# Block sums of resident operands made beforehand, in pieces, and the last item's evacuations ahead of the rows behind it

## The chip, the cores and the metric

The kernel runs on one core of a Trainium2 chip. A core has five engines that work through their own lists of instructions in order: TensorE (PE, matrix products, with its weight loads listed as PEld), VectorE (DVE), ScalarE (ACT), GpSimd (POOL) and SyncE (SP), which issues most transfers. Waiting between engines goes by semaphores. Transfers (DMA) move data between device memory (DRAM tensors in the program) and the on-chip memory, and TensorE writes its results into banks of a separate accumulator memory (PSUM). The metric is device time in microseconds of one execution.

## The reference

One residual layer on a sequence of 2,048 positions with 1,024 channels: a mixer (eight heads of attention with forget gates beside a gated MLP on chunks of 128 positions), a dense SwiGLU network with 2,816 hidden channels, and a final norm.

```python
for l in range(DEPTH):                                    # DEPTH = 1
    xn = rms_norm(x, mix_norm_g[l])
    h = xn @ w_in[l]
    ...                                                   # attention and spatial gating
    x = x + merged @ w_out[l]
    xn = rms_norm(x, ffn_norm_g[l])
    gate, up = jnp.split(xn @ w_gate_up[l], 2, axis=-1)
    x = x + (jax.nn.silu(gate) * up) @ w_down[l]
return rms_norm(x, final_norm_g)
```

The change touches only the last four lines, the feed-forward part. Everything is float32; the kernel writes each float32 operand as a high half (a cast) and a low half (the rest), and makes a product of two such operands as three matmuls (high-high, high-low, low-high).

## The kernel before

The feed-forward part is the second half of the program, from about 1,098 us to the end. It works on *sets*: sets 1 and 2 are the gate-and-up products for the first and the second half of the positions (22 items each, one item per 128 hidden channels), sets 3, 4 and 5 the down product, cut into three blocks of hidden channels (8 items each, an item being two tiles of 128 positions). Two items at a time make a *group*; only the last two groups have one item each. Counted from 0, set 1 is groups 0 to 10, set 2 is 11 to 21, set 3 is 22 to 25, set 4 is 26 to 29 and set 5 is 30 to 34.

Within an item the product of two matrices is done by blocks, two by two, with seven block products in place of eight (Winograd's scheme). Each product n, from 0 to 6, takes one *moving-side* operand from the item's own stream (tiles `wh`, `wl`, made from the loaded tiles `raw`, `rawd`) and one *resident* operand that stays for the whole set (R0 to R6, each with a high and a low half; R0, R2, R5 and R6 live in the long tiles named `wh` and `wl` of 4,096 columns, R1, R3 and R4 in tiles of their own). Some of these operands are blocks of the matrices, others are sums of blocks. `stream` makes the sums and halves of an item. `refill` makes the resident ones of the next set while the last group of the current set runs: after product n of that group its resident operand is free, and the next set's operand n is written in its place (`keep_as`: a cast on ScalarE, line 128, and a low half on VectorE, line 131, both over 2,048 columns).

Before the change, the four blocks of the next set lie in four staging slots `sg0` to `sg3` of 1 MB each (loaded at lines 1327 and 1331), and the block sums are made there in place, on VectorE (line 1343, 128x2048; one of those for set 5 on GpSimd): one at product 4 of the group before the last, three in the last group, between the casts:

```python
yield keep(0, b11)
tt(te[1], b11, b11, b12, ALU.add)
yield keep(1, b11)
yield keep(2, b21)
tt(te[2], b21, b21, b11, ALU.subtract)
tt(te[3], b11, b22, b11, ALU.subtract)
yield keep(3, b11)
```

Order is set by the program's own loop over (group, product) slots and by a scheduler that places each engine's instructions; every engine then runs its list in order. Moving-side operands are made ahead of TensorE, up to six (item, product) pairs (`LW = 6`), in six buffers for each half. Results leave PSUM in `evac`: for sets 1 and 2 (class `Up`) into `u`, `c` and `hT`, stored to DRAM at line 1472 (`HD`), for sets 3 to 5 (class `Down` on `Rows`) into rows of x that are loaded at line 1404 and stored at 1510. In set 5 a finished row is squared (line 1506), its reciprocal root is taken (VectorE at line 177, GpSimd at 179), it is scaled (line 1531) and stored (line 1532). These steps (`done`) wait in a list `posts`, and the main loop takes one step per item and product. The last matmuls are those of group 34, and the rows of group 33 finish beside it.

Lines that the prediction names: 1654 is the matmul of all seven products, 1409 and 1411 the evacuation of products 0 and 1 of a row item, 1414, 1416, 1418, 1421 and 1424 that of products 2 to 6; 1439 and 1484 load an item's raw tiles, 1466 and 1470 are GpSimd's products of the gate.

## Time and profile before

| | us |
|---|---|
| three runs | 2388.26 to 2390.97, median 2390.56 |
| the profiled execution | 2384.64 |
| its span, first to last instruction | 2382.8 |
| TensorE busy | 2338.7 (98%) |
| VectorE busy | 1671.5 (70%) |
| ScalarE busy | 1055.9 (44%) |
| GpSimd busy | 627.4 (26%) |
| granted TensorE clock, mean | 0.995 of full |

The transfers move 380.6 MB at a mean of 160 GB/s. Shares are averages over stages that differ: what counts is the busy time of each engine group by group, and which wait ends last where TensorE stands idle. Matmul records overlap, since a matmul starts before the one ahead of it has ended; so a full TensorE is read from the distance of starts, or from the count of matmuls in a window.

### The profile page before, as it was taken

What the parts mean: (1) busy time and instruction counts of PE and PEld (TensorE: products, weight loads), DVE (VectorE), ACT (ScalarE), POOL (GpSimd) and SP (SyncE); (2) the same over time, 40 slices, a digit from 0 to 9 for tenths busy, and PEclk for the clock granted to TensorE, in tenths of its full rate; (3) what the DMA queues carried; (4) which work ended last, traced back from release to release, by engine and by line L of the source; (5) the groups of instructions that cost most, each with busy time, mean ns of one, the idle gap of its engine ahead of it and who ended that gap; (6) DMA issues with size and microseconds to landing.
All of it is one profiled execution on the core that took longest, in us unless ns stands there. A gap on an engine that the chain in (4) does not pass through costs nothing. (4 is left out here: it accounts for less than half of the span.)

```text
span 2382.8 us, 31420 instructions
## 1 busy us (share of the span) xinstructions
PE 2338.7 (98%) x10582; PEld 1893.8 (79%) x10582; DVE 1671.5 (70%) x2736; ACT 1055.9 (44%) x1770; POOL 627.4 (26%) x705
## 2 busy tenths in 40 slices
PE   9999999999999999999999999999999999999997
PEld 7777777777777767888888888788888878888886
DVE  6658658888888666567655656965555696696888
ACT  5322137777778766344323233432323242332433
POOL 1100002122111222221322323232322335364531
PEclk9999999999999999999999999999999999999999
DMA  7845567566587876666233232433232245455453
GB/s 256 286 154 202 196 210 196 165 164 178 154 222 234 225 224 172 211 223 201 71 89 89 80 95 75 153 85 89 72 89 81 81 140 187 167 185 202 152 188 148
DMA packets 358152, 380.60 MB, mean 160 GB/s; under 512 B 22292, under 2 KB 275924, under 8 KB 355432
## 3 DMA queue, kind: packets, MB, share of 16 engines
q1 hardware_dynamic: 342008, 335.36, 46.4%
q0 software_dynamic: 7616, 27.33, 3.3%
q10 hardware_dynamic: 8368, 15.91, 1.8%
q8 instruction: 85, 1.39, 0.2%
q14 instruction: 75, 0.61, 0.1%
HBM read 253.35 MB, written 125.18 MB: 159 GB/s over the span
## 5 line engine op out<-in xcount | busy, mean ns | idle before, releaser
L128 ACT CAST wh<-raw 128x512 fp32r<-128x512 f32 (+2 forms) x492 | 302.3, 621 | 752.7 <-PE pp L1654 607.9
L131 DVE TENSOR_TENSOR wl<-raw,wh 128x512 fp32r<-128x512 f32 (+2 forms) x496 | 374.9, 766 | 80.2 <-ACT wh L128 79.8
L1654 PE MATMUL pp<-wl,wh 128*128 128x512 f32 x1056 | 325.5, 389 | 1.4 <-ACT u L1409 1.2
L1654 PE MATMUL pp<-wh,wh 128*128 128x512 f32 x1056 | 325.3, 389 | 0.0
L1343 POOL TENSOR_TENSOR raw<-raw 128x512 f32<-128x512 f32 (+1 forms) x124 | 165.5, 1336 | 514.9 <-DMA raw<-in_w_gu_dram 334.9
L131 DVE TENSOR_TENSOR Pl<-Pt,Ph 128x512 fp32r<-128x512 f32 (+1 forms) x320 | 194.6, 613 | 79.1 <-ACT Ph L128 76.4
L1654 PEld LDWEIGHTS pp<-wl,wh 128*128 128x128 f32 x1056 | 198.0, 188 | 43.6 <-ACT u L1409 2.1
L1654 PEld LDWEIGHTS pp<-wh,wh 128*128 128x128 f32 x1056 | 198.2, 188 | 41.1
L732 ACT ACTIVATE Pt<-mx_ps 128x512 f32<-128x512 f32 (+1 forms) x320 | 169.3, 534 | 121.6 <-PE mx_ps L730 117.6
L1654 PE MATMUL pp<-wl,wl 128*128 128x512 f32 x528 | 205.7, 390 | 1.0 <-DVE wl L131 0.9
L1654 PE MATMUL pp<-wh,wl 128*128 128x512 f32 x528 | 205.4, 389 | 0.0
L921 PE MATMUL z<-wh,xz 128*128 128x512 f32 x496 | 188.9, 397 | 0.0
L1343 DVE TENSOR_TENSOR raw<-raw,raw 128x512 f32<-128x512 f32 (+1 forms) x112 | 133.8, 1197 | 77.4 <-POOL raw L1343 73.9
L128 ACT CAST Ph<-Pt 128x512 fp32r<-128x512 f32 (+1 forms) x320 | 175.8, 557 | 19.6 <-PE tp L764 3.8
L365 DVE TENSOR_REDUCE mx<-mx_ps 128x1 f32<-128x512 f32 x192 | 130.2, 682 | 23.9 <-PE mx_ps L363 20.4
L742 POOL TENSOR_SCALAR_AFFINE_SELECT Ph<-Ph 128x128 fp32r<-128x128 f32 x128 | 53.0, 414 | 323.0 <-DVE Pl L131 218.6
L363 PE MATMUL mx_ps<-D,A 66*128 66x512 f32 (+2 forms) x320 | 119.6, 376 | 5.7 <-DMA D<-KH 3.0
L762 PE MATMUL tp<-Ph,V 128*128 128x512 f32 (+1 forms) x320 | 118.6, 371 | 4.5 <-POOL Ph L742 3.6
L729 PE MATMUL mx_ps<-A,D 74*128 74x512 f32 (+1 forms) x320 | 118.9, 372 | 2.2 <-ACT Pt L732 2.2
L767 PE MATMUL tp<-Pl,V 128*128 128x512 f32 (+1 forms) x320 | 118.5, 370 | 1.2 <-POOL Pl L742 0.7
L1654 PEld LDWEIGHTS pp<-wl,wl 128*128 128x128 f32 x528 | 99.1, 188 | 22.6 <-DVE wl L131 2.1
L730 PE MATMUL mx_ps<-B,C 128*128 128x512 f32 (+1 forms) x320 | 116.9, 366 | 0.0
(340 smaller groups left out, 5300.9 us busy)
## 6 DMA issues: line engine op xcount, KB each, us to landing
raw<-in_w_gu_dram SPq DMA_DIRECT2D x88, 512.0 KB
xz<-XS SPq DMA_DIRECT2D x31, 1024.0 KB
HD<-hT SPq DMA_DIRECT2D x44, 512.0 KB
D<-KH SPq DMA_DIRECT2D x112, 128.0 KB
XA<-xa SPq DMA_DIRECT2D x27, 512.0 KB
raw<-HD SPq DMA_DIRECT2D x24, 512.0 KB
XA<-xb SPq DMA_DIRECT2D x21, 512.0 KB
xa<-XA SPq DMA_DIRECT2D x20, 512.0 KB
```

The costliest lines, as they stand in the source:

```text
L128: return nc.scalar.copy(o, i) if eng is nc.scalar else eng.tensor_copy(o, i)
L131: return eng.tensor_tensor(o, i, f(h), ALU.subtract)
L363: last_mx.append(nc.tensor.matmul(pm[:, 0:n], lhs, Dt[0 : lhs.shape[0], 0:n], start=True, stop=True))
L365: nc.vector.tensor_reduce(mx[:, a, s : s + 1], pm, AX.X, ALU.max)
L729: nc.tensor.matmul(st[:, off:], Dt[:, b * P : (b + 1) * P], A[:, off:], start=True, stop=False)
L730: nc.tensor.matmul(st[:, off:], C[:, b * P : (b + 1) * P], B[:, off:], start=False, stop=True)
L732: nc.scalar.activation(Pt[:, off:], st[:, off:], AF.Exp)
L762: nc.tensor.matmul(pv[:, off:], V[:, 0:P], Ph[:, off:], start=kb == 0, stop=False)
L767: nc.tensor.matmul(pv[:, off:], V[:, 0:P], Pl[:, off:], start=False, stop=kb == 4 * j + 3)
L921: nc.tensor.matmul(pz, xz[a][:, k, :], w[b][:, k, :], start=n == 0, stop=n == 3 * KT - 1)
L1343: (nc.vector if e == "v" else nc.gpsimd).tensor_tensor(o, a, b, op)
L1654: nc.tensor.matmul(pm, a[:, k, :], b[:, k, :], start=on is None and k == 0 and e == 0, stop=k == it.kh - 1 and e == 2, skip_group_check=n ...
```

## The change

The block sums of sets 2 to 5 are no longer made in the staging slots. A generator `block_sums` makes them beforehand, in 15 pieces (four for sets 2, 3 and 4, three for set 5), one in each of the groups 1 to 15: it loads a piece of 512 columns of each of the four blocks (256 KB each) into two tiles `xa`, makes four sums on VectorE (128x512), and stores the two tiles to new DRAM tensors `SM` (512 KB each), behind the group's two output stores. In the slot loop, the next set's slots are filled with operands 0 to 3, which are now either a block or a stored sum; in the last group, `refill` only casts and takes low halves, and after each of operands 0, 1 and 2 loads operand 4, 5 or 6 into the slot that has just been read.

For the last group alone, the steps of finished rows are taken in other numbers per product (two each for products 0 to 3, none for product 4, one for 5 and 6), they are placed behind the product's evacuation (`behind`), and in that group a row's reciprocal root and its scaling become two steps.

```diff
@@ -53,7 +53,6 @@
 NF_ = 6
 RL = 2
 SQ = 'p'
-TE = ['vvvv', 'vvpv', 'vvvv', 'vvvv', 'vvvv', 'vvpv']
 SE = 'pvpv'
 NY = 4
 NR = 5
@@ -1319,19 +1318,74 @@
     def stage():
         return [T(pers, [P, 4, CH], F32, f"sg{n}") for n in range(4)]
 
+    def block(s, i):
+
+        if s < 3:
+            return XT[s - 1][i]
+        kh, r0 = KB[s - 3] // 2, sum(KB[: s - 3])
+        r0 = (r0 + (i // 2) * kh) * P
+        return w_down[r0 : r0 + kh * P, (i % 2) * CH : (i % 2 + 1) * CH].rearrange("(k p) n -> p k n", p=P)
+
     def staged(s):
 
         sg = stage()
         for i, t in enumerate(sg):
-            if s < 3:
-                ld(t, XT[s - 1][i])
-                continue
-            kh, r0 = KB[s - 3] // 2, sum(KB[: s - 3])
-            r0 = (r0 + (i // 2) * kh) * P
-            ld(t[:, 0:kh, :],
-               w_down[r0 : r0 + kh * P, (i % 2) * CH : (i % 2 + 1) * CH].rearrange("(k p) n -> p k n", p=P))
+            ld(t, block(s, i))
         return sg
 
+    SM = {s: T(dram, [P, 4, 4, CH], F32, f"SM{s}") for s in (2, 3, 4, 5)}
+
+    def source(s, n):
+
+        if n in (0, 2, 6):
+            return block(s, {0: 0, 2: 2, 6: 3}[n])
+        return SM[s][:, {1: 0, 4: 1, 5: 2, 3: 3}[n], 0 : sets[s - 1][0].kh]
+
+    def fetch(s, n):
+
+        t = T(pers, [P, 4, CH], F32, f"sg{n % 4}")[:, 0 : sets[s - 1][0].kh]
+        ld(t, source(s, n))
+        return t
+
+    hd = []
+
+    def block_sums():
+
+        last = None
+        for s in (2, 3, 4, 5):
+            for k in range(sets[s - 1][0].kh):
+                n = yield
+                while n != 2:
+                    n = yield
+                if last:
+                    with behind(hd[-1]):
+                        put(*last)
+                while n != 3:
+                    n = yield
+                t = [T(xap, [P, D], F32, "xa") for _ in range(2)]
+                b = [t[i // 2][:, (i % 2) * CH : (i % 2 + 1) * CH] for i in range(4)]
+                with behind(*hd[-1:]):
+                    for i in range(4):
+                        ld(b[i], block(s, i)[:, k])
+                while n != 5:
+                    n = yield
+                tt("v", b[1], b[3], b[1], ALU.subtract)
+                tt("v", b[0], b[0], b[1], ALU.add)
+                n = yield
+                tt("v", b[2], b[2], b[0], ALU.subtract)
+                tt("v", b[3], b[3], b[0], ALU.subtract)
+                last = s, k, t
+        while n != 2:
+            n = yield
+        with behind(hd[-1]):
+            put(*last)
+        yield
+
+    def put(s, k, t):
+        for a in range(2):
+            ld(SM[s][:, 2 * a : 2 * a + 2, k], t[a].rearrange("p (c n) -> p c n", c=2))
@@ -1340,7 +1394,7 @@
     JOIN = {2: 0, 6: 3}
 
     def tt(e, o, a, b, op):
-        (nc.vector if e == "v" else nc.gpsimd).tensor_tensor(o, a, b, op)
+        return (nc.vector if e == "v" else nc.gpsimd).tensor_tensor(o, a, b, op)
 
     def keep_as(i, src, kh=4):
         rh, rl = resident(i)
@@ -1348,23 +1402,14 @@
         lo_of(nc.vector, rl[:, 0:kh, :], src, rh[:, 0:kh, :])
         return rh, rl
 
-    def refill(sg, kh, te):
-
-        b11, b12, b21, b22 = (t[:, 0:kh, :] for t in sg)
-
-        def keep(i, src):
-            return keep_as(i, src, kh)
-
-        yield keep(0, b11)
-        tt(te[1], b11, b11, b12, ALU.add)
-        yield keep(1, b11)
-        yield keep(2, b21)
-        tt(te[2], b21, b21, b11, ALU.subtract)
-        tt(te[3], b11, b22, b11, ALU.subtract)
-        yield keep(3, b11)
-        yield keep(4, b12)
-        yield keep(5, b21)
-        yield keep(6, b22)
+    def refill(s, sg):
+
+        kh = sets[s - 1][0].kh
+        for n in range(7):
+            r = keep_as(n, sg[n], kh)
+            if n < 3:
+                sg.append(fetch(s, n + 4))
+            yield r
 
     def stream(a11, a12, a21, a22):
 
@@ -1409,19 +1454,19 @@
                 copies.append(nc.scalar.copy(u, ps[0]))
             elif n == 1:
                 nc.vector.tensor_tensor(u, u, ps[1], ALU.add)
-                tt(self.adder, x[0][1], x[0][1], u, ALU.add)
+                self.last = tt(self.adder, x[0][1], x[0][1], u, ALU.add)
...
             for m in {5: (1,), 6: (0,)}.get(n, ()):
                 posts.append(self.done(2 * self.tp + m, self.x[m], now[0]))
 
@@ -1469,8 +1514,8 @@
                 nc.scalar.activation(h1, u, AF.Silu)
                 nc.gpsimd.tensor_tensor(h1, h1, c, ALU.mult)
                 kb, r = [(i, j) for i in range(3) for j in range(KB[i])][self.fi]
-                ld(HD[kb][self.half * 8 : (self.half + 1) * 8, :, r, :].rearrange("b p t -> p b t"),
-                   self.h.rearrange("p q (b t) -> p (q b) t", t=P))
+                hd[:] = [ld(HD[kb][self.half * 8 : (self.half + 1) * 8, :, r, :].rearrange("b p t -> p b t"),
+                            self.h.rearrange("p q (b t) -> p (q b) t", t=P))]
 
     class Down(Rows):
         def __init__(self, kb, tp):
@@ -1528,6 +1573,8 @@
                 self.squares(xt, ss)
             yield
             r = rsqrt(pev, ss, 1.0 / D, "r4")
+            if at == len(grp) - 1:
+                yield
             nc.vector.scalar_tensor_tensor(xt, xt, r, finb, ALU.mult, ALU.mult)
             ld(o, xt)
             yield
@@ -1622,6 +1669,8 @@
     make()
     load(1)
     nextR = [None] * 7
+    sums = block_sums()
+    next(sums)
     for q in range(len(slots)):
         p, n = slots[q]
         s, i, its, last = grp[p]
@@ -1630,14 +1679,11 @@
             if s == 5:
                 finb = T(pers, [P, 4, CH], F32, "sg0")[:, 0:2, :].rearrange("p a n -> p (a n)")
                 ld(finb, fin_g.rearrange("(o n) -> o n", o=1).broadcast_to([P, D]))
-        if n == 0 and i == 2 and s < 5:
-            sg = staged(s + 1)
+        if n == 0 and i == max(2, len(sets[s - 1]) - 8) and s < 5:
+            sg = [fetch(s + 1, m) for m in range(4)]
         last = last and s < 5
-        if n == 4 and s < 5 and i + 2 * len(its) == len(sets[s - 1]):
-            b = [t[:, 0 : sets[s][0].kh, :] for t in sg]
-            tt(TE[s + 1][0], b[1], b[3], b[1], ALU.subtract)
         if n == 0 and last:
-            fill = refill(sg, sets[s][0].kh, TE[s + 1])
+            fill = refill(s + 1, sg)
         while nq < len(slots) and len(made) + len(grp[slots[nq][0]][2]) <= LW:
             make()
         if n == 0:
@@ -1662,11 +1708,20 @@
                 it.evac(m)
         if n == 0:
             now[0] = p
-        for _ in range(len(its)):
-            while posts and next(posts[0], 0) == 0:
-                posts.pop(0)
+        tail = p == len(grp) - 1
+        with behind(*[its[0].last] if tail and n else ()):
+            for _ in range((2, 2, 2, 2, 0, 1, 1)[n] if tail else len(its)):
+                while posts and next(posts[0], 0) == 0:
+                    posts.pop(0)
+            if tail and n == 6:
+                next(posts.pop(), None)
         if last:
             nextR[n] = next(fill)
+        if sums and p:
+            try:
+                sums.send(n)
+            except StopIteration:
+                sums = None
     finish(posts)
     estk.close()
```

The following rows show the order at the three places that matter. A row is: line, operation, output<-inputs, shape; a name's last number is the buffer. (Line numbers in the changed kernel are its own.)

VectorE in the last group of set 1, before. `sg` on the left are block sums, `R4l`, `R3l`, `wh_12296` low halves of resident operands 4, 3 and 5, `raw` on the left the small sums of the next group's items.

```order
L131 TENSOR_TENSOR R1l_15227<-sg_3283_12612,R1h_15226 128x2048
...
L131 TENSOR_TENSOR wl_12191<-sg_3285_12614,wl_12191 128x2048
L1460 TENSOR_TENSOR c_15181<-u_15180,pp_15287 128x512
L1343 TENSOR_TENSOR sg_3285_12614<-sg_3285_12614,sg_3283_12612 128x2048
L131 TENSOR_TENSOR wl_15309<-raw_3705_15051,wh_15308 128x512
L1343 TENSOR_TENSOR sg_3283_12612<-sg_3286_12615,sg_3283_12612 128x2048
...
L131 TENSOR_TENSOR R4l_15347<-sg_3284_12613,R4h_15346 128x2048
L131 TENSOR_TENSOR R3l_15305<-sg_3283_12612,R3h_15304 128x2048
...
L131 TENSOR_TENSOR wh_12296<-sg_3285_12614,wh_12296 128x2048
L1343 TENSOR_TENSOR raw_3759_15350<-raw_3760_15352,raw_3759_15350 128x512
L1343 TENSOR_TENSOR raw_3761_15354<-raw_15356,raw_3761_15354 128x512
```

The same place now (`xa` are the piece's sums):

```order
L1397 TENSOR_TENSOR xa_15422<-xa_15423,xa_15422 128x512
L130 TENSOR_TENSOR R1l_15337<-sg_3588_14368,R1h_15336 128x2048
L130 TENSOR_TENSOR wl_15383<-raw_3728_15158,wh_15382 128x512
L1397 TENSOR_TENSOR xa_15422<-xa_15422 128x512
L130 TENSOR_TENSOR wl_15387<-raw_15162,wh_15386 128x512
L1397 TENSOR_TENSOR xa_15423<-xa_15423,xa_15422 128x512 x2
L130 TENSOR_TENSOR wl_12195<-sg_3589_14370,wl_12195 128x2048
...
L130 TENSOR_TENSOR R3l_15419<-sg_3590_14372,R3h_15418 128x2048
...
L130 TENSOR_TENSOR R4l_15467<-sg_3753_15294,R4h_15466 128x2048
...
L1397 TENSOR_TENSOR raw_3786_15470<-raw_3787_15472,raw_3786_15470 128x512
L1397 TENSOR_TENSOR raw_3788_15474<-raw_15476,raw_3788_15474 128x512
L130 TENSOR_TENSOR wh_12300<-sg_3762_15340,wh_12300 128x2048
```

The three sums of 2,048 columns are gone, four of 512 have come, R3's low half stands ahead of R4's, and the next group's small sums stand ahead of the low half of operand 5.

SyncE's queue over the same stretch, before:

```order
L1472 DMA HD_142_205<-hT_14894 128x8x128
L1472 DMA HD_142_205<-hT_14898 128x8x128
L1439 DMA raw_3760_15352<-in_w_gu_dram 128x8x128
L1439 DMA raw_15356<-in_w_gu_dram 128x8x128
L1439 DMA raw_3761_15354<-in_w_gu_dram 128x8x128
L1439 DMA raw_15634<-in_w_gu_dram 128x8x128
L1331 DMA sg_3822_15725<-in_w_down_dram 128x4x512
```

and now:

```order
L1517 DMA HD_142_205<-hT_14996 128x8x128
L1386 DMA SM_2993_11126<-xa_15112 128x2x512
L1386 DMA SM_2993_11126<-xa_15113 128x2x512
L1369 DMA xa_15422<-in_w_down_dram 128x512 x2
L1369 DMA xa_15423<-in_w_down_dram 128x512 x2
L1347 DMA sg_3753_15294<-SM_2991_11124 128x2048
L1347 DMA sg_3762_15340<-SM_2991_11124 128x2048
L1484 DMA raw_3787_15472<-in_w_gu_dram 128x8x128
L1484 DMA raw_15476<-in_w_gu_dram 128x8x128
L1347 DMA sg_3767_15378<-XT_123_186 128x2048
L1484 DMA raw_3788_15474<-in_w_gu_dram 128x8x128
L1484 DMA raw_15766<-in_w_gu_dram 128x8x128
```

Between the output stores and the next raw loads stand a piece's stores and loads, and two of the three reloads of slots; the third reload stands in the middle of the raw loads.

VectorE in group 34, before (`pp` are PSUM banks; `sg_4930` holds the last item's rows, `sg_4894` the rows of group 33):

```order
L1411 TENSOR_TENSOR u_21847<-u_21847,pp_21859 128x512
L177 TENSOR_SCALAR r4a_21884<-ss_4937_21871 128x1
L1343 TENSOR_TENSOR sg_4930_21844<-sg_4930_21844,u_21847 128x512
L1531 SCALAR_TENSOR_TENSOR sg_4894_21697<-sg_4894_21697,r4r_21886,sg_4715_20896 128x1024
L1414 TENSOR_TENSOR sg_4930_21844<-sg_4930_21844,pp_21834 128x512
L1416 TENSOR_TENSOR sg_4930_21844<-sg_4930_21844,pp_21890 128x512
L1501 TENSOR_SCALAR a_4942_21901<-a_4942_21901 128x1
L1502 TENSOR_TENSOR sg_4930_21844<-sg_4930_21844,sg_4715_20896 128x512
L177 TENSOR_SCALAR r4a_21921<-ss_4944_21906 128x1
L1531 SCALAR_TENSOR_TENSOR sg_4894_21697<-sg_4894_21697,r4r_21923,sg_4715_20896 128x1024
L1418 TENSOR_TENSOR u_21847<-u_21847,pp_21909 128x512
```

and now (`sg_4976` the last item's rows, `sg_4940` those of group 33):

```order
L1456 TENSOR_TENSOR u_22039<-u_22039,pp_22054 128x512
L1397 TENSOR_TENSOR sg_4976_22036<-sg_4976_22036,u_22039 128x512
L176 TENSOR_SCALAR r4a_22066<-ss_4980_22047 128x1
L1459 TENSOR_TENSOR sg_4976_22036<-sg_4976_22036,pp_22026 128x512
L1578 SCALAR_TENSOR_TENSOR sg_4940_21889<-sg_4940_21889,r4r_22068,sg_4761_21088 128x1024
L176 TENSOR_SCALAR r4a_22085<-ss_4987_22072 128x1
L1546 TENSOR_SCALAR a_4992_22102<-a_4992_22102 128x1
L1547 TENSOR_TENSOR sg_4976_22036<-sg_4976_22036,sg_4761_21088 128x512
L1578 SCALAR_TENSOR_TENSOR sg_4940_21889<-sg_4940_21889,r4r_22087,sg_4761_21088 128x1024
L1461 TENSOR_TENSOR sg_4976_22036<-sg_4976_22036,pp_22091 128x512
L1463 TENSOR_TENSOR u_22039<-u_22039,pp_22107 128x512
```

The second row's reciprocal root now stands directly behind the first row's scaling, ahead of `a` (which waits for a square of product 2's result), and product 3 has moved behind the second row's scaling. On ScalarE the squares of the second row and of `a` have changed places. From product 4 on the two lists are the same.

10 lines of the change are left out of this document (5 added, 5 removed).

## The prediction

> **What bounds the kernel now.** I read the stages first (a table of windows), then TensorE's own timeline for its gaps, then the engine named behind each gap. In the table one row is one group of products; "x" counts instructions.
>
> ```profile
> core 0: us, PE busy (x) PEld busy (x) DVE busy (x) ACT busy (x) POOL busy (x), PEclk, DMA share, GB/s
> 1289.00:1327.00 38.00, 38.00 (x170) 31.46 (x169) 21.99 (x30) 11.84 (x20) 10.81 (x9) 1.00 0.29 84
> 1482.00:1520.00 38.00, 38.00 (x169) 31.50 (x168) 34.68 (x30) 20.14 (x22) 6.71 (x6) 1.00 0.34 96
> 1520.00:1558.00 38.00, 36.41 (x158) 29.19 (x158) 35.81 (x40) 14.21 (x23) 17.07 (x10) 1.00 0.58 182
> 1941.70:1980.00 38.30, 33.41 (x137) 26.20 (x136) 34.43 (x36) 12.81 (x20) 21.57 (x13) 0.96 0.64 218
> 2108.00:2146.00 38.00, 37.06 (x163) 30.33 (x162) 32.32 (x34) 10.46 (x18) 20.50 (x13) 1.00 0.60 211
> ```
>
> The first row is an ordinary group: TensorE full, 170 matmuls touching 38 us (about 0.227 us each, with the two at the edges taken off), VectorE busy 22.0 us. The second is the last group of set 1, in which the next set's resident operands are made: VectorE 34.7 of 38. The other three are the first groups of sets 2, 3 and 4, and there matmuls are missing: against 169 to 170, 11.5, 33.5 and 6.5 of them, which times 0.227 is 2.6, 7.6 and 1.5 us. The feed-forward part is bound by TensorE everywhere except behind these changes of set. Its timeline shows the same as gaps:
>
> ```profile
> 1527.07 0.50 PE L1654 MATMUL pp<-R1h,wh 128*128 128x512 f32 x1 [1.18 <-ACT wh L128]
> 1948.47 0.50 PE L1654 MATMUL pp<-R1h,wh 128*128 128x512 f32 x1 [1.24 <-ACT wh L128]
> 1957.62 0.50 PE L1654 MATMUL pp<-R3h,wl 128*128 128x512 f32 x1 [2.32 <-DVE wl L131]
> 2114.14 0.50 PE L1654 MATMUL pp<-wl,wl 128*128 128x512 f32 x1 [0.94 <-DVE wl L131]
> ```
>
> Added up start to start over all matmuls behind these changes, the excess is 2.4, 7.5 and 1.2 us, 11.1 in all; behind the fourth (near 2266 us) it is 0.1. I use 11.1, the smaller of the two counts. TensorE waits for moving operands (wh, wl) whose halves come late, and why they are late stands on VectorE and ScalarE:
>
> ```profile
> 1493.97 2.28 DVE L1343 TENSOR_TENSOR sg<-sg,sg 128x2048 f32<-128x2048 f32 x1
> 1505.99 3.04 DVE L1343 TENSOR_TENSOR sg<-sg,sg 128x2048 f32<-128x2048 f32 x1
> 1509.56 2.28 DVE L1343 TENSOR_TENSOR sg<-sg,sg 128x2048 f32<-128x2048 f32 x1
> ...
> 1521.56 3.06 DVE L131 TENSOR_TENSOR wh<-sg,wh 128x2048 fp32r<-128x2048 f32 x1
> 1524.54 2.37 DVE L1343 TENSOR_TENSOR raw<-raw,raw 128x512 f32<-128x512 f32 x2
> 1526.40 1.74 ACT L128 CAST wh<-raw 128x512 fp32r<-128x512 f32 x3 [4.00 <-DVE raw L1343]
> ```
>
> The sums of 2,048 columns are the block sums that the change moves. VectorE works in order without a gap, so ScalarE's cast waits 4.00 us for the small sum at 1524.54, and TensorE for the cast.
>
> **The change, part by part.**
>
> (1) *Block sums out of the last groups.* Before the first gap lie three of the four sums: 2.28 + 3.04 + 2.28 = 7.6 us of VectorE. The last group of set 1 gets one piece instead, four adds of 128x512; the two such adds at 1524.54 took 2.37 us together beside GpSimd and about 0.69 each alone, so the four are 2.8 to 4.7 us, and I take 2.8, since GpSimd is idle where they stand. The new order also puts the small sum ahead of the 3.06 us low half at 1521.56. So it comes 7.6 - 2.8 + 3.1 = 7.9 us earlier at best, and some waits come in. The walk through the new order, with steps from start to start of 2.2 us for 2,048 columns and 0.6 for 512: the low half of R1 ends at 1501.0 (row in part 2); two low halves and three adds to 1504.0; R2's to 1506.2; four small ones to 1508.6; R3's, whose cast ends at 1509.1, to 1511.3; five small ones to 1514.3; R4's to 1516.5; three small ones to 1518.3; the two small sums to 1520.1; R5's (3.06 beside GpSimd, as above) to 1523; the two low halves of product 1 at 1523.6 and 1524.2. TensorE wants the first at 1525.7 (1527.07 less its wait and start). The gap of 1.2 us goes with some 2 us to spare. Behind sets 2 and 3 no piece is added (there are 15 pieces, in groups 1 to 15), so VectorE is 6.6 to 7.6 us ahead and the spare is of the same size. Saving 11.1 us; for what is left over (the walk is tight at 1941.7) I take off 0.5. Bounds: 0, if something else is late by as much, and 11.7.
>
> The largest of the three holds a part that is not waiting:
>
> ```profile
> 1957.60:1962.00 4.40, 4.38 (x12) 3.48 (x13) 4.19 (x6) 1.77 (x3) 1.10 (x1) 0.61 0.76 249
> ```
>
> Twelve matmuls where 19.4 fit, at a granted clock of 0.61: 7.4 times 0.227, so 1.7 of the 7.5 us, are a slower clock right behind the 2.32 us gap. I take it that it goes with the gap. The Trainium skill ("TensorE: Matmul & The Clock Gate", "What's actually happening") lets the clock fall only after an idle window of about 3.4 us; here the longest gap is 2.32 us, so by that rule these 1.7 us would have another cause and could stay, and the sum would be 10.2 instead of 11.9. The trace puts the slow stretch directly behind the longest gap, so the measurement decides for me, with a chance left for the rule below.
>
> (2) *Refetch in the last group.* Slots 0, 1 and 2 are reloaded (1 MB each) once their low halves are read, and casts of what arrives follow. The rows on which this hangs:
>
> ```profile
> 1490.57 2.29 DVE L131 TENSOR_TENSOR wh<-sg,wh 128x2048 fp32r<-128x2048 f32 x1 [0.85 <-ACT wh L128]
> 1498.74 2.29 DVE L131 TENSOR_TENSOR R1l<-sg,R1h 128x2048 fp32r<-128x2048 f32 x1 [0.68 <-ACT R1h L128]
> 1502.14 3.33 DVE L131 TENSOR_TENSOR wl<-sg,wl 128x2048 fp32r<-128x2048 f32 x1
> ...
> 1509.61 1.92 ACT L128 CAST R4h<-sg 128x2048 fp32r<-128x2048 f32 x1 [2.33 <-PE pp L1654]
> 1515.05 1.92 ACT L128 CAST wh<-sg 128x2048 fp32r<-128x2048 f32 x1 [0.68 <-PE pp L1654]
> 1955.25 0.51 SPq L1331 DMA_DIRECT2D sg<-in_w_down_dram  x1
> 1961.87 2.29 DVE L1343 TENSOR_TENSOR sg<-sg,sg 128x2048 f32<-128x2048 f32 x1 [0.21 <-DMA sg<-in_w_down_dram]
> ```
>
> The last two give the price of such a load under traffic: 1961.87 - 1955.25 = 6.6 us. The slots are free at 1492.9, 1501.0 and, with the waits above, about 1506.6; the loads land at 1499.5, 1507.6 and 1513.2. TensorE does not release the targets before 1509.6, 1515.0 and 1520.3, so 7 to 10 us remain. Queued behind these waits on SyncE's queue are the next group's operand loads: the third load, in front of the cast for the second item of the next group, goes from about 1503 to 1507 and lands 4 us later (next fence), at 1511, where that cast stands at 1514 to 1515. Cost taken: nothing. Without this cover it is the lateness itself, at most some 4 us per change of set.
>
> (3) *Pieces in groups 1 to 15.* Each brings four loads of 256 KB, two stores of 512 KB and the four adds. The stores stand behind the group's two output stores and the next loads into the same two tiles wait for them:
>
> ```profile
> 1293.22 4.74 SPq L1472 DMA_DIRECT2D HD<-hT  x2
> 1306.76 8.97 SPq L1439 DMA_DIRECT2D raw<-in_w_gu_dram  x4
> 1310.77 1.29 POOL L1343 TENSOR_TENSOR raw<-raw 128x512 f32<-128x512 f32 x1 [13.21 <-DMA raw<-in_w_gu_dram]
> 1305.38 0.62 ACT L128 CAST wh<-raw 128x512 fp32r<-128x512 f32 x1 [2.10 <-PE pp L1654]
> 1306.04 0.69 DVE L131 TENSOR_TENSOR wl<-raw,wh 128x512 fp32r<-128x512 f32 x1 [1.86 <-ACT wh L128]
> SPq L1404 <- DMA XA<-xa: 44.0, 17, 4.6
> ```
>
> SyncE is idle from 1298.0 to 1306.8, where stores and loads fit. A reload waits for a 512 KB store 44.0 / 17 = 2.6 us on average and 4.6 at most; a 512 KB load lands 1310.77 - 1306.76 = 4.0 us after issue. So stores at 1298.4, loads from 1301 to 1304, data at 1305.5 to 1308. The adds stand in VectorE's order in front of the low half that now starts at 1306.04, and are reached at 1304.1: VectorE, which works in order, then waits 1.4 to 4 us for the data in each group and does 2.8 us of adds. Behind it wait the low halves, the raw loads that they release (1306.76 becomes about 1310) and GpSimd's sum. What hides it: casts are made when TensorE releases one of six buffers, five products of 2.72 us ahead, 13.6 us, less 1.3 for cast and low half, so 12.3 us against 4 + 2.8 = 6.8. VectorE's load rises to 22.0 + 6.8 = 28.8 of 38. Cost: nothing.
>
> (4) *The tail.* The last item's evacuations no longer queue behind finished rows' scaling.
>
> ```profile
> 2369.96 0.39 PE L1654 MATMUL pp<-wl,wl 128*128 128x512 f32 x1
> 2358.89 1.06 ACT L1506 ACTIVATE jk<-sg 128x1024 bf16<-128x1024 f32 x1
> 2367.06 0.63 ACT L1506 ACTIVATE jk<-sg 128x512 bf16<-128x512 f32 x1 [7.02 <-issue]
> 2366.30 0.68 DVE L1414 TENSOR_TENSOR sg<-sg,pp 128x512 f32<-128x512 f32 x1
> 2369.00 0.15 DVE L177 TENSOR_SCALAR r4a<-ss 128x1 f32<-128x1 f32 x1 [0.43 <-ACT jk L1506]
> 2369.88 1.28 DVE L1531 SCALAR_TENSOR_TENSOR sg<-sg,r4r,sg 128x1024 f32<-128x1024 f32 x1 [0.73 <-POOL r4r L179]
> 2371.08 0.68 DVE L1418 TENSOR_TENSOR u<-u,pp 128x512 f32<-128x512 f32 x1
> ```
>
> TensorE ends at 2370.35 with product 6 (products are counted from 0; one of this item takes 2.04 us); product 4, done by 2366.3, is taken up only at 2371.08, behind a row that waited for ScalarE (idle 7.02 us before) and GpSimd. In the new order the second finished row is squared straight after the first, near 2360 to 2362; the chain on VectorE becomes: adds of product 1 to 2364.5, reciprocal root of the first row and product 2 to 2365.3, its scaling 2365.8 to 2367.0, the second row's root at 2367.1, its scaling 0.9 us later (as 2369.00 to 2369.88) to 2369.2, product 3 to 2369.8, and product 4 at 2369.8 instead of 2371.08. What follows is the same list, so 1.3 us come off the end. Bounds: 0 and 2.
>
> **Sum.** 11.1 - 0.5 + 1.3 = 11.9 us. The profiled execution took 2384.64 us (span 2382.8), so it would take 2372.7. It lies 5.9 us below the median of the timed runs, 2390.56, which I cannot attribute; I carry the difference over: 2390.6 - 11.9 = **2378.7 us**.
>
> **The rivals.** *Half the stalls stay* because the refetch, the raw loads and the pieces' traffic meet (DMA share is 0.58 to 0.64 in these stages already): ScalarE and VectorE then wait in order for a late tile. For it: three extra megabytes in 20 us; against: 7 to 10 us to spare. 11.1 / 2 + 1.3 = 6.9, so 2383.7. *The wait only changes its name*: all of the stall comes back as waiting for tiles, 1.3 us are left, 2389.3; against it stands that VectorE is the full engine in the table and no load is. *The slow clock stays* where it is, whatever the gap in front of it does: 11.9 - 1.7 = 10.2, so 2380.4; against it, no other stretch of this part shows one. (That would be the skill's rule above.) *The pieces break the cover*: where the data land more than about 9.5 us after VectorE reaches the adds (12.3 less 2.8), that is later than 1313.6, every further microsecond is one of TensorE's in each of 14 groups; at one microsecond that is 14 - 11.9, so 2392.7. The distance is 5.6 us from the latest landing that I work out. The Trainium skill ("GPSIMD Engine Reference", its specification table) has VectorE contend with GpSimd for SBUF where it reads two inputs there; the pair at 1524.54 agrees (2.37 instead of 1.4 us), and late adds would meet GpSimd's sum at 1310.77 and take some 4.7 instead of 2.8, which makes this rival a little likelier but not its bound.
>
> **How the numbers follow.** Forecast 0.60, with its own range of 2375 to 2382; slow clock stays 0.07; half stays 0.15; name only 0.10; cover broken 0.08. A measurement of this kernel tells about 0.2% (4.8 us) from no change, so faster means below 2385.8: 0.60 + 0.07 + two thirds of 0.15, so 0.77; same 0.05 + 0.10, so 0.15; slower 0.08. The range runs from 2373.5 (all of 11.7 and 2 in the tail, and 3 more if a slow stretch of clock falls away in the timed runs that the profile did not have) to 2388, which leaves out the last two rivals, 0.18.
>
> **What would show it.** Right: first groups of sets 2 to 4 with 169 or 170 matmuls in 38 us and a granted clock of 1.00; the last group of set 1 with VectorE well below 34.7 us apart from waits; waits of VectorE for DMA of the piece tiles of 1 to 4 us in groups 2 to 15 and none on TensorE; casts from the refetched slots still released by TensorE; the end 12.4 - 1.3 = 11.1 us behind TensorE's last matmul. Wrong: TensorE waiting in the middle of set 1 or 2, casts of R4, R5 or R6 released by a DMA, or a raw load that lands after its cast's turn.

## The result

The changed kernel takes 2378.6 us (median of seven runs, 2375.5 to 2382.8), the kernel before, on the same chip, 2388.3 us: ratio 0.9961, 95% interval 0.9947 to 0.9974. Run once more later, it came to 0.9966 (0.9952 to 0.9980). It is faster by 0.34 to 0.39%, some 8 to 9 us, and the forecast of 2378.7 us is met. Three of its terms are not: the waits behind set 2 and the pieces cost more than forecast, and the end gave more.

The profiled execution has a span of 2373.6 us, 9.2 less than before. Two rows cut it in three: the last transposes ahead of the feed-forward part, and the start of TensorE's last matmul. Here the first row of the kernel before (its last matmul, 2369.96, stands in the prediction), then TensorE's timeline of the changed kernel:

```profile
1099.28 1.07 PE L1153 MATMUL tp<-ident,xn 128*128 128x128 f32 x8 [0.48 <-DVE xn L1146]
```

```profile
1098.21 1.07 PE L1152 MATMUL tp<-ident,xn 128*128 128x128 f32 x8 [0.48 <-DVE xn L1145]
...
1571.13 0.82 PE L1700 MATMUL pp<-wl,wh 128*128 128x512 f32 x2 [2.71 <-ACT u L1499]
1571.75 0.63 PE L1700 MATMUL pp<-wl,wl 128*128 128x512 f32 x1
...
1955.10 0.50 PE L1700 MATMUL pp<-R3h,wl 128*128 128x512 f32 x1 [0.82 <-DVE wl L130]
1961.39 0.73 PE L1700 MATMUL pp<-wl,wh 128*128 128x512 f32 x2 [0.97 <-ACT u L1454]
...
2364.32 0.39 PE L1700 MATMUL pp<-wl,wl 128*128 128x512 f32 x1
```

Of the 9.2 us, 1.1 lie ahead of the first row, in work that the change does not touch. From the first row to the last TensorE needs 1266.1 us in place of 1270.7, and the end behind the last matmul shrinks from 12.8 to 9.3. I call the middle part *TensorE's stretch*; all later runs are compared by it, since it leaves out what happens before 1098 us. The waits behind the changes of set are gone but for two, at 1955 and 1961. A new one stands at 1571, 53 us into set 2, with half the clock behind it. The same in the table of windows, whose rows are the ordinary group, the last group of set 1, the first two groups of set 2 and the first groups of sets 3 and 4:

```profile
core 0: us, PE busy (x) PEld busy (x) DVE busy (x) ACT busy (x) POOL busy (x), PEclk, DMA share, GB/s
1289.00:1327.00 38.00, 38.00 (x169) 31.45 (x168) 24.45 (x35) 11.73 (x20) 10.78 (x8) 1.00 0.63 194
1482.00:1520.00 38.00, 38.00 (x169) 31.45 (x169) 30.59 (x34) 19.46 (x21) 9.72 (x7) 1.00 0.82 261
1520.00:1558.00 38.00, 38.00 (x169) 31.29 (x168) 29.90 (x34) 13.71 (x22) 11.23 (x6) 1.00 0.66 210
1558.00:1596.00 38.00, 35.29 (x150) 28.70 (x149) 23.29 (x34) 10.79 (x19) 12.23 (x9) 0.96 0.47 139
1941.70:1980.00 38.30, 36.51 (x160) 29.57 (x159) 32.60 (x35) 12.94 (x20) 20.46 (x13) 1.00 0.54 183
2108.00:2146.00 38.00, 38.00 (x169) 31.48 (x168) 27.34 (x35) 9.68 (x16) 15.52 (x11) 1.00 0.69 244
```

The first groups of sets 2 and 4 are full (169 matmuls), the one of set 3 has 160, and the second group of set 2 has 150. The DMA share in an ordinary group is more than twice that of before (0.63 against 0.29), and no matmul is missing there.

Where the new wait comes from is read backward from 1571: TensorE waits for ScalarE's copy (L1499), which stands behind late casts, and these behind late weights and late sums on VectorE. The rows of the engines, in the order of the cause: GpSimd, SyncE, VectorE, ScalarE.

```profile
1527.39 4.98 POOL L1397 TENSOR_TENSOR raw<-raw 128x512 f32<-128x512 f32 x2 [5.83 <-DVE wl L130]
1532.33 3.44 POOL L1515 TENSOR_TENSOR hT<-hT,c 128x512 f32<-128x512 f32 x2
...
1292.15 4.73 SPq L1517 DMA_DIRECT2D HD<-hT  x2
1534.10 2.06 SPq L1517 DMA_DIRECT2D HD<-hT  x2
1536.21 1.94 SPq L1386 DMA_DIRECT2D SM<-xa  x2
1538.25 1.21 SPq L1347 DMA_DIRECT2D sg<-in_w_down_dram  x1
1540.58 2.94 SPq L1369 DMA_DIRECT2D xa<-in_w_down_dram  x4
1543.61 11.37 SPq L1484 DMA_DIRECT2D raw<-in_w_gu_dram  x4
...
1309.70 0.69 DVE L1397 TENSOR_TENSOR xa<-xa,xa 128x512 f32<-128x512 f32 x1 [6.60 <-DMA xa<-in_w_down_dram]
1548.50 0.69 DVE L1397 TENSOR_TENSOR xa<-xa,xa 128x512 f32<-128x512 f32 x1 [7.98 <-DMA xa<-in_w_down_dram]
...
1556.32 0.62 ACT L127 CAST wh<-raw 128x512 fp32r<-128x512 f32 x1 [12.02 <-DMA raw<-in_w_gu_dram]
1570.50 0.58 ACT L1499 COPY u<-pp 128x512 f32<-128x512 f32 x1
```

The rows at 1292.15 and 1309.70 are those of an ordinary group. Six groups of 168 matmuls (38.09 us each by the start-to-start step of 0.2267) are 228.5 us, so the store in group 11, the first of set 2, would be due at 1520.7. It goes at 1534.10, 13.4 us late. GpSimd does two additions of weights (4.98 us) ahead of the product that the store carries, and comes to them itself only at 1527.39, when VectorE has made a low half. The piece's loads stand behind this store. VectorE comes to the piece's first sum at 1540.5 (1548.50 less its wait; in the ordinary group at 1303.1, which would be 1531.6), waits 7.98 us for the data, and everything behind it waits too: the low halves, the raw tiles that they release, ScalarE's casts of the next weights.

A large part of this lateness stood in the profile of before. Its store in group 11:

```profile
1530.07 3.66 SPq L1472 DMA_DIRECT2D HD<-hT  x2
```

Counted from 1293.22 (in the prediction) by the same six groups, it was due at 1521.7 and went 8.3 us late, with GpSimd's two additions behind the products there. In the changed kernel they stand ahead of them.

### The profile page after: what moved, and what is told of

Same layout as the page of the kernel before. It is cut to its first block, busy times and chain, and to the rows that moved or that the text cites. A ratio compares the mean times of both kernels' runs of the same rounds, so it can differ in the third digit from the quotient of the medians.

```text
span 2373.6 us, 31663 instructions
## 1 busy us (share of the span) xinstructions
PE 2337.4 (98%) x10582; PEld 1894.0 (80%) x10582; DVE 1671.6 (70%) x2781; ACT 1056.5 (45%) x1770; POOL 611.6 (26%) x704
## 5 line engine op out<-in xcount | busy, mean ns | idle before, releaser
L1397 POOL TENSOR_TENSOR raw<-raw 128x512 f32<-128x512 f32 (+1 forms) x124 | 172.6, 1394 | 568.6 <-DMA raw<-in_w_gu_dram 363.1
```

Of the source, the lines that this page charges most:

```text
L1397: return (nc.vector if e == "v" else nc.gpsimd).tensor_tensor(o, a, b, op)
```

## The experiments

I held three theories of the 4.6 us at 1571: (H) the late store, behind which the piece's loads stand; (Q) the 1 MB reloads for set 3 that stand ahead of them in SyncE's list, and their traffic; (A) the sums' own work on VectorE. Besides, the runs ask whether the sums caused the old waits, what the new order at the end is worth by itself, and what the last two waits come from. All results in one table; the ratio is against the kernel before, run on the same chip. The start is that of the last transposes, the stretch goes from there to the last matmul's start, the end from there to the span's end. Excess is start to start on TensorE over the step of 0.2267 us.

| run | median us | ratio (95%) | start | stretch | end | excess in set 2 | excess at set 3 |
|---|---|---|---|---|---|---|---|
| before | 2388.3 | | 1099.3 | 1270.7 | 12.8 | 2.4 | 7.6 |
| changed | 2378.6 | 0.9961 (0.9947-0.9974) | 1098.2 | 1266.1 | 9.3 | 4.6 | 2.4 |
| skip | 2374.2 | 0.9953 (0.9941-0.9965) | 1099.4 | 1261.3 | 9.3 | 0 | 2.3 |
| late | 2379.5 | 0.9975 (0.9964-0.9986) | 1102.0 | 1265.9 | 9.7 | 4.6 | 2.2 |
| delay | 2376.1 | 0.9958 (0.9946-0.9970) | 1105.2 | 1262.4 | 9.3 | 1.0 | 2.4 |
| nopiece | 2374.3 | 0.9950 (0.9937-0.9962) | 1103.4 | 1261.5 | 9.4 | 0 | 2.5 |
| store | 2373.9 | 0.9949 (0.9935-0.9963) | 1097.4 | 1261.3 | 9.3 | 0 | 2.2 |
| nosums | 2374.0 | 0.9947 (0.9931-0.9963) | 1102.1 | 1260.4 | 11.4 | 0 | 1.8 |
| tailonly | 2382.8 | 0.9987 (0.9978-0.9997) | 1100.3 | 1269.4 | 9.6 | 2.5 | 6.1 |
| oldtail | 2380.8 | 0.9977 (0.9968-0.9987) | 1103.9 | 1265.7 | 11.1 | 4.8 | 2.3 |
| storeaddv | 2377.3 | 0.9960 (0.9948-0.9973) | 1101.4 | 1260.4 | 10.2 | 0.1 | 1.3 |
| again (changed) | 2378.3 | 0.9966 (0.9952-0.9980) | 1103.2 | 1264.0 | 9.2 | 2.7 | 2.3 |

The column "start" varies by 7.8 us between executions, in work that none of these kernels changes there. That alone is as much as the whole effect, so medians and ratios say little between two variants, while the stretch tells them apart. The last four columns come from one profiled execution each: the changed kernel's two stretches differ by 2.1 us, 1.7 of them a stretch of slow clock, and the ends of all kernels with the new order lie between 9.2 and 10.2.

**skip: no piece in group 11.** That piece and those behind it, four of them, each move one group on.

```diff
+                if (s, k) == (4, 2):
+                    n = yield
+                    while n != 2:
+                        n = yield
                 while n != 3:
                     n = yield
                 t = [T(xap, [P, D], F32, "xa") for _ in range(2)]
```

> The changed kernel with no piece in the first group of set 2 (group 11): that piece and the three behind it each move one group on; nothing is left out. In the changed kernel TensorE stands 2.71 us at 1571 and then runs at half clock, 4.6 us together. Three theories. (H) the loads of that piece go out late, because the store of the group's outputs ahead of them in SyncE's order is 13.5 us late there, and VectorE, in order, stands 7.98 us at the piece's first sum: the wait at 1571 goes, the sums of the moved pieces find their data as in the other groups, and the kernel takes about 2374.0 (2378.6 - 4.6). (Q) the same wait, but caused by the 1 MB reload that stands ahead of the piece in SyncE's order and by its traffic: the same 2374.0 here. (A) the four sums themselves, 2.7 us of VectorE at a place where it has no room: also gone here, but part of it would come back in group 12, where the next piece now meets the same VectorE backlog: 2375 to 2378. If the wait at 1571 stays, the pieces are not its cause: 2378.6.

The stretch falls by 4.8 us to 1261.3, the wait at 1571 is gone and none comes back in group 12. So a piece in group 11 makes it, and (A) is out in its strong form: the sums that moved to the groups behind cost nothing there. (H) and (Q) are both still open.

**late: the reloads for set 3 moved away.**

```diff
-            sg = [fetch(s + 1, m) for m in range(4)]
+            with behind(*hd[-1:] if s == 2 else ()):
+                sg = [fetch(s + 1, m) for m in range(4)]
```

> The changed kernel with the four 1 MB reloads for set 3 ordered behind the stores of group 17 in place of going out at 1512 to 1539, so that none stands in SyncE's order ahead of the piece of group 11 and none lands beside it; nothing is left out. (Q) the reloads are the cause: the piece's loads go out about when the stores do, land in 4 to 5 us, the 7.98 us wait of VectorE shrinks below 3 us, the wait of TensorE at 1571 goes, about 2374.0. (H) the store of the outputs ahead of them stays 13.5 us late: the loads go out 1.2 us earlier (the reload's own time in the order), land a little sooner, VectorE still waits 4 to 7 us, and TensorE's wait at 1571 shrinks but stays, 1 to 4 us of the 4.6: 2375 to 2378. (A) the sums' own work: 2378.6.

SyncE's list in group 11 of this run, VectorE's first sum and TensorE's two waits:

```profile
1537.62 2.06 SPq L1517 DMA_DIRECT2D HD<-hT  x2
1539.73 1.94 SPq L1386 DMA_DIRECT2D SM<-xa  x2
1544.14 2.21 SPq L1369 DMA_DIRECT2D xa<-in_w_down_dram  x4
...
1550.31 0.69 DVE L1397 TENSOR_TENSOR xa<-xa,xa 128x512 f32<-128x512 f32 x1 [6.86 <-DMA xa<-in_w_down_dram]
1554.21 0.50 PE L1701 MATMUL pp<-wh,wl 128*128 128x512 f32 x1 [0.71 <-DVE wl L130]
1576.42 0.73 PE L1701 MATMUL pp<-wl,wh 128*128 128x512 f32 x2 [3.29 <-ACT u L1499]
```

This execution starts its stretch 3.7 us later than the changed kernel's. Taken off, the store goes at 1533.9 and the loads at 1540.4, against 1534.1 and 1540.6: with no reload in between, the loads wait for the stores of the piece before, which free their tiles. The data land 1.9 us sooner, VectorE still waits 6.86 us, and the excess is 4.6 us as before, now 1.0 at 1554 and 3.6 at 1576 with no slow clock behind it. So the reloads do not make the wait, and (Q) is out; (H) had allowed at most 4 of the 4.6. One thing more than the reloads changed: in this kernel VectorE does three of the piece's sums ahead of the next low half where the changed kernel does two, and it is for that low half that TensorE waits at 1554.

**delay: the piece's sums later on VectorE.** All four stand behind the group's product 5; the two others are held in the same way.

```diff
-                tt("v", b[1], b[3], b[1], ALU.subtract)
-                tt("v", b[0], b[0], b[1], ALU.add)
+                held = [its[-1].v5] if (s, k) == (4, 2) else []
+                with behind(*held):
+                    tt("v", b[1], b[3], b[1], ALU.subtract)
+                    tt("v", b[0], b[0], b[1], ALU.add)
                 n = yield
...
-                nc.vector.tensor_tensor(h1, h1, ps[5], ALU.add)
+                self.v5 = nc.vector.tensor_tensor(h1, h1, ps[5], ALU.add)
```

> The changed kernel with the four sums of group 11's piece ordered on VectorE behind its work on the group's product 5, some 11 instructions later, the loads left where they are; nothing is left out. (H) and (Q) both say that VectorE then finds the data landed (it landed at 1548.5; the sums come after about 1550): the 7.98 us wait goes, the raw weights behind it come in time, no wait of TensorE at 1571, about 2374.0. (A) the same 2.7 us of sums are still done in this group: the wait stays or moves some us on, 2377 to 2379. If the raw weights' loads, which go out only behind the piece's loads, are late by themselves, ScalarE's 12.02 us wait for them and TensorE's wait stay too: 2378.6.

The wait at 1571 is gone, with the same loads, the same store and the same four sums in the group. What harms is therefore not the sums but standing in order in front of data that have not landed. 1.0 us came back in group 13:

```profile
1560.79 1.14 ACT L127 CAST wh<-raw 128x512 fp32r<-128x512 f32 x2 [9.53 <-DMA raw<-in_w_gu_dram]
...
1614.12 0.73 PE L1703 MATMUL pp<-wl,wh 128*128 128x512 f32 x2 [0.73 <-ACT u L1502]
```

ScalarE still waits 9.53 us for the raw tiles (12.02 in the changed kernel), so a part of the lateness, small enough to be covered in this group, hangs on the late loads and not on VectorE's wait.

**nopiece: no pieces at all.** The refill reads bare blocks; the block sums are left out.

```diff
-        return SM[s][:, {1: 0, 4: 1, 5: 2, 3: 3}[n], 0 : sets[s - 1][0].kh]
+        return block(s, {0: 0, 2: 2, 6: 3, 1: 0, 4: 1, 5: 2, 3: 3}[n])
...
-    sums = block_sums()
-    next(sums)
+    sums = None
```

> The changed kernel without the pieces: no loads, sums or stores of block sums; the refill reads the bare blocks in place of the sums, so the products are of other operands (the sums are left out). The changed tail and the seven loads per refill stay. My theory: the pieces cost only the 4.6 us at 1571; the 2.4 us that TensorE still stands in the first group of set 3 (1955 to 1961) have another cause and stay, and so does the tail: about 2374.0, TensorE's last matmul about 2359.7 in the profiled run. Rival 1: the pieces also load VectorE, GpSimd and the DMA engines elsewhere and cost more than that one wait: below 2373. Rival 2: the wait at 1571 does not come from the pieces: 2378.6.

1261.5 us against 1261.3 with all fifteen pieces and only those from group 11 on moved: 15 MB read, 15 MB written and some 41 us of VectorE's work cost TensorE nothing in the executions seen, except in group 11. The waits at set 3 stay (2.5 us), so they are not the pieces' doing.

**store: GpSimd's two additions taken from in front of the late store.** Two additions for group 11's weights go to VectorE (the edit is in class `Up`).

```diff
-    def stream(a11, a12, a21, a22):
+    def stream(a11, a12, a21, a22, se=SE):
...
-            self.ops = stream(*self.raw)
+            self.ops = stream(*self.raw, se='pvvv' if self.half == 1 and self.fi < 2 else SE)
```

> The changed kernel with two additions of weights for group 11's own products (128x512 each) on VectorE in place of GpSimd; nothing is left out. In the changed kernel these two take GpSimd 4.98 us from 1527.39 and stand ahead of the multiplication whose result the late store carries (1532.33, store at 1534.10). My theory, after the runs before this one: the wait at 1571 goes back to that late store, behind which the piece's loads stand. Then the multiplication starts behind ScalarE's activation, which ends at 1527.43, the store goes out at about 1531, the loads 3 us sooner, VectorE's wait for them falls from 7.98 to about 4 to 5 us, and TensorE's wait at 1571 goes or falls below 1 us: TensorE's stage from its first matmul of the two halves on 1262 instead of 1266, about 2374.5. Rival: the two additions cost VectorE more than the sooner store gives, since VectorE is the one that is behind there: the wait at 1571 stays above 2 us, 2377 to 2380.

```profile
1525.63 3.25 POOL L1515 TENSOR_TENSOR hT<-hT,c 128x512 f32<-128x512 f32 x2 [5.36 <-ACT hT L1514]
1527.20 2.06 SPq L1517 DMA_DIRECT2D HD<-hT  x2
1533.69 2.87 SPq L1369 DMA_DIRECT2D xa<-in_w_down_dram  x4
1541.57 0.69 DVE L1397 TENSOR_TENSOR xa<-xa,xa 128x512 f32<-128x512 f32 x1 [3.33 <-DMA xa<-in_w_down_dram]
1558.00:1596.00 38.00, 38.00 (x170) 31.45 (x169) 24.63 (x35) 11.84 (x21) 11.37 (x9) 1.00 0.46 138
```

This execution starts 0.8 us earlier; with that, the store goes 6.1 us sooner, twice what I had expected, VectorE's wait falls from 7.98 to 3.33 us, and group 12 has its 170 matmuls. The stretch is 1261.3 us, that of the run without pieces. Take away what GpSimd does ahead of the store, and the wait at 1571 goes, pieces and sums staying where they are. The store is still 7.3 us late by the count above; that much the group bears. The edit does a second thing: without GpSimd's pair beside them VectorE's 128x512 operations there take 0.68 us and not 1.77, so it does not pay for the two additions and comes to the sums 1.5 us sooner. But its wait ends 6.2 us sooner, as much as the loads go out sooner (6.1). With delay, where the loads stayed and VectorE's turn moved, (H) is shown: late loads, and VectorE standing in order in front of them.

**nosums: the kernel before without the sums in its refill.** These sums are left out; the products are of bare blocks.

```diff
-        tt(te[1], b11, b11, b12, ALU.add)
-        tt(te[2], b21, b21, b11, ALU.subtract)
-        tt(te[3], b11, b22, b11, ALU.subtract)
...
-            tt(TE[s + 1][0], b[1], b[3], b[1], ALU.subtract)
```

> The kernel before with VectorE's sums of blocks between the splits of the refill taken out (for sets 2 to 5; 128x2048 and 128x1536 operations; the products are of bare blocks and the result is another). Tail, loads and stores are as before. My theory: these sums alone make the waits of TensorE behind the changes of set; without them TensorE's 2.4 us behind set 1 and its 1.2 us behind set 3 go, and of the 7.5 us behind set 2 some 2.4 stay, as in the changed kernel. TensorE's stage from its first matmul of the up projection to its last falls from 1270.7 to about 1261.6 us, as in the run without pieces (1261.5), the tail stays at 12.8, the kernel takes about 2379. Rival: the waits come from the refill as such (the splits, the loads' landing) and stay: 1270.7, 2388.

The stretch falls by 10.3 us, a little more than expected; behind sets 1 and 3 nothing is left, at set 3's first group 1.8 us. So VectorE's block sums made the old waits, 5.8 of the 7.6 us behind set 2 among them. The median is 2374.0 us where I had expected 2379. The end was 11.4 and not 12.8 us, without any new order: see the next two runs.

**tailonly and oldtail: the new order at the end alone, and all but it.** Each has one half of the change:

```diff
+        tail = p == len(grp) - 1
+        with behind(*[its[0].last] if tail and n else ()):
+            for _ in range((2, 2, 2, 2, 0, 1, 1)[n] if tail else len(its)):
+                while posts and next(posts[0], 0) == 0:
+                    posts.pop(0)
...
```

> The kernel before with the change's new order at the end alone (no pieces, the old refill); nothing is left out. In the changed kernel the span ends 9.3 us behind the start of TensorE's last matmul, before 12.8. My theory: the new order itself gives 1.4 us (the time from the sum of product 1 to that of product 4 fell from 7.84 to 6.45 us); the other 2 us came from VectorE's and ScalarE's lead over TensorE at the end, which the kernel before does not have: 11.4 us here, ratio to the kernel before 0.9994. Rival 1: the order gives all of it, 9.3 us, ratio 0.9985. Rival 2: without that lead the order gives nothing, since other work on VectorE is late by as much: 12.8 us.

> The changed kernel with the old order at the end; nothing is left out. My theory: the new order is worth 1.4 us by itself: the span ends 10.7 us behind the start of TensorE's last matmul in place of 9.3, about 2380. Rival 1: it is worth all of the 3.5 us that the tail got shorter: 12.8 us, about 2382. Rival 2: the lead of VectorE does it alone: 9.3 us, 2378.6. In each case TensorE's stage before stays at 1266.1 us.

The chain that the prediction walked runs from the sum of product 1 to that of product 4. Its first and last row in the old order (before, oldtail), then in the new one (tailonly, changed):

```profile
2363.24 0.68 DVE L1411 TENSOR_TENSOR u<-u,pp 128x512 f32<-128x512 f32 x1
2371.08 0.68 DVE L1418 TENSOR_TENSOR u<-u,pp 128x512 f32<-128x512 f32 x1
...
2361.47 0.68 DVE L1456 TENSOR_TENSOR u<-u,pp 128x512 f32<-128x512 f32 x1
2369.30 0.68 DVE L1463 TENSOR_TENSOR u<-u,pp 128x512 f32<-128x512 f32 x1
```

```profile
2361.20 0.68 DVE L1411 TENSOR_TENSOR u<-u,pp 128x512 f32<-128x512 f32 x1
2367.65 0.68 DVE L1418 TENSOR_TENSOR u<-u,pp 128x512 f32<-128x512 f32 x1
...
2355.76 0.68 DVE L1456 TENSOR_TENSOR u<-u,pp 128x512 f32<-128x512 f32 x1
2362.21 0.68 DVE L1463 TENSOR_TENSOR u<-u,pp 128x512 f32<-128x512 f32 x1
```

7.84 and 7.83 us in the old order, 6.45 and 6.45 in the new: 1.4 us. The end shrank by 1.8 us from oldtail to the changed kernel, but 0.4 of this is TensorE's last matmul coming later (it waits a little for product 3's sum in the new order), so 1.4 are left. The other part of the 3.5 us is very likely not the change's: in the one profiled execution of the kernel before, VectorE begins the chain 6.7 us ahead of TensorE's last matmul, in oldtail 8.1, and tailonly, whose work ahead of its last group is that of the kernel before, has 8.5 (0.7 of these are a wait of TensorE's own there). VectorE fell behind in that one execution well ahead of the end, where tailonly and the kernel before are the same program. From 2226 to 2268 tailonly is 0.35 us ahead of before; then GpSimd waits for a load of rows of x (before, then tailonly):

```profile
2274.02 1.30 POOL L1343 TENSOR_TENSOR xa<-xa,u 128x512 f32<-128x512 f32 x1 [2.30 <-DMA xa<-XA]
2272.01 1.29 POOL L1343 TENSOR_TENSOR xa<-xa,u 128x512 f32<-128x512 f32 x1 [0.81 <-DMA xa<-XA]
```

Less the 0.35, that is 1.7 us later in before; VectorE's addition to the same tile comes as much later, and the first row of the chain (2363.24 against 2361.20) is still 1.7 us late. Why the load was late was not studied. My theory's 11.4 us for tailonly was wrong for this reason: 9.6, near the 9.3 of the rival that gave all of it to the order. Its 10.7 for oldtail was nearly right (11.1). The timed runs do not decide: the ratio for the order alone, 0.9987 (0.9978 to 0.9997), is 3.1 us, with an interval of 0.7 to 5.3.

**storeaddv: the two waits at set 3.** As store, and the same for the first two items of the first down set (the edit is in class `Down`).

```diff
-            self.ops = stream(*self.raw)
+            self.ops = stream(*self.raw, se='pvvv' if self.kb == 0 and self.tp < 2 else SE)
```

> The kernel of the run on the late store (two additions of group 11's weights on VectorE) with the same two additions of the first down-projection group (group 22) on VectorE as well; nothing is left out. TensorE still waits twice there, 0.7 to 0.9 us for VectorE's split of weights and 0.97 us for ScalarE's copy, each with a dearer matmul behind it, 2.2 to 2.4 us together. My theory: the first wait comes from VectorE's operations that run beside GpSimd's two additions (3.38 us for a 128x2048 split that takes 2.28 alone, 1.77 for a 128x512 one that takes 0.68): with the additions on VectorE the first wait goes, the second stays, since ScalarE's copy stands behind a cast that itself waits for TensorE: TensorE's stage 1260.2 us in place of 1261.3, time about 2372.9 or 0.5 to 1 below the other. Rival 1: VectorE is simply full there, and two additions more make the first wait longer: 1262 to 1263. Rival 2: both waits hang together and go: 1259.

```profile
1947.78 3.37 DVE L130 TENSOR_TENSOR wl<-sg,wl 128x2048 fp32r<-128x2048 f32 x1
1951.08 0.68 DVE L1397 TENSOR_TENSOR raw<-raw 128x512 f32<-128x512 f32 x1
...
1958.86 0.73 PE L1700 MATMUL pp<-wl,wh 128*128 128x512 f32 x2 [1.02 <-ACT u L1454]
```

As the theory had it: the first wait goes, the second stays, 1260.4 us. Only a part of its mechanism held, though: the 128x512 operations fell to 0.68 us, while the 128x2048 split still took 3.37, now beside GpSimd's products of the gate. The median is 4.4 us above the 2372.9 expected. The time cannot tell this kernel from the changed one (0.9960 and 0.9966, measured side by side, intervals overlapping); TensorE's stretch is 3.6 us shorter than that of the changed kernel beside it. Of the kernels that leave nothing out, store has the lowest ratio, 0.9949 against 0.9961 and 0.9966 of the changed kernel, and its interval overlaps theirs too.

**again: the changed kernel once more.**

> The changed kernel once more, unaltered, beside the run with the four moved additions, for a comparison on one chip. Expected from the runs so far: the wait at 1571 is there again, 2.7 to 3.3 us, with or without half clock behind it (4.6 or 3.4 us in all); TensorE's stage 1265 to 1266 us, 4 to 6 us longer than with the additions moved; a time of 2378 to 2379.

The wait at 1571 is there again (2.42 us), this time without half clock behind it, and the stretch is 1264.0 us, 1 us below the range expected.

## Why the prediction was right, and where not

**Block sums out of the last groups** (predicted 11.1 us less 0.5 left over). Right in cause, as nosums shows, and right to 0.1 us behind sets 1, 3 and 4 (2.4, 1.2 and 0.1). Behind set 2, 2.4 of the 7.6 us stayed, not 0.5. Behind set 1 the walk was closer than it looked: the two small sums end at 1522.1 (1518.95 plus 3.16), not at 1520.1, because they run beside GpSimd's products, and the 2 us to spare were about used up. That walk had been made for the change from set 1 to set 2 and was carried over to the others; at set 3 GpSimd's two additions stretch VectorE's operations (1.77 for 0.68 us), and ScalarE's copy stands behind a cast that waits for TensorE itself. The first was in the rows before (2.37 us for a pair); the second, 0.97 us, was in the profile of before at the same place (1965.48). It is in nosums too, so it does not come from the sums; that it comes from the cast ahead of it is read from the rows, no run took it away.

**The slow clock** (1.7 us, taken to go with its gap). It went: the gap at 1957 is gone, and 1955 to 1962 runs at full clock. But a slow stretch came back behind the new gap, and late has a longer gap with none behind it, so it is partly luck that this term held (more in the last section):

```profile
1571.20:1574.70 3.50, 3.50 (x9) 2.73 (x10) 3.36 (x4) 2.02 (x4) 1.35 (x2) 0.56 0.37 97
```

**The refetch** (cost nothing, some 7 us to spare). Right: among ScalarE's waits from 1098 us on none is for a reload of a staging slot, and the first groups of sets 2 and 4 are full. But one of the prediction's own signs of being wrong did show, a raw load that lands after its cast's turn. In the last group of set 1:

```profile
1515.54 0.62 ACT L127 CAST wh<-raw 128x512 fp32r<-128x512 f32 x1 [5.09 <-DMA raw<-in_w_gu_dram]
```

The third and fourth raw load go at 1509.26, not by 1507, and the third lands at 1515.5, not at 1511, behind the turn of its cast (1514 to 1515 in the prediction). None of it reached TensorE.

**The pieces** (cost nothing). This is the step with the wrong mechanism, though only in one group of fifteen. The cover was worked out for an ordinary group: 12.3 us against 4 of waiting and 2.8 of sums. Even there the wait was 6.60 us, not 1.4 to 4, since the data landed at 1309.7, 1.7 us beyond my latest; with the sums that made 9.4 of 12.3. In the fourteen groups other than group 11 VectorE's wait was 3.5 to 7.2 us, and they bore it. The longest of these, in group 13:

```profile
1621.45 0.69 DVE L1397 TENSOR_TENSOR xa<-xa,xa 128x512 f32<-128x512 f32 x1 [7.16 <-DMA xa<-in_w_down_dram]
```

The 7.98 us of group 11 are only 0.8 more, and with 2.7 of sums still below 12.3; so it is not the length of the wait that broke the cover, but that the cover was gone when the wait began. In group 11 VectorE came to the sums 8.9 us later in the group, because the last refill's splits stand there and run beside GpSimd's additions, and the data came 10.3 us later, because the store ahead of them was late. I had taken the moment of the loads from where SyncE was idle in group 5, and had not followed the store back through GpSimd in the group where all engines are behind. The rival "the pieces break the cover" had the mechanism, but put it in all groups; it was one, 2.7 to 4.8 us in the executions seen. Its price, one microsecond of TensorE for each beyond the cover, is not borne out: its latest moment, 1313.6, is 1541.0 in group 11 (228.5 later, less the 1.1 by which this execution is ahead), the data came 7.5 us after that, and TensorE lost 2.9 us waiting and 1.7 to the slow clock.

**The tail** (1.3 us). The chain got 1.4 us shorter, as walked. The predicted end, 11.1 us behind the end of the last matmul and so 11.5 behind its start, was 9.3; with the old order the changed kernel has 11.1 and nosums 11.4, so the 12.8 that I had started from were very likely those of an execution whose VectorE was late.

**The sum.** By terms: 2.4 + 5.2 + 1.2 + 0.1 behind the sets, 0.5 for a small wait near 2345 that is gone, less 4.6 at 1571 and 0.4 near the end: 4.4 of the 4.6 us by which the stretch shrank; 3.5 at the end, 1.1 ahead of it all, together 9.2 against the 11.9 predicted. Of these 9.2, the 1.1, some 1.7 of the end and the 0.5 near 2345 (tailonly does not have that wait either) are not the change's; about 6 us are traced to it, half of what was predicted and at the low end of the two comparisons' intervals (6 to 13 and 5 to 11 us). Whether the change saves more than that stays open. That the forecast of 2378.7 is met to 0.1 us is in good part chance. The medians show a saving of 9.7 us, 2.2 less than predicted, and the median of the kernel before came out at 2388.3 in this comparison, 2.3 us below the one that I started from.
